# Softmax times V: the last head of each pass is normalised inside the loop's final branch, with stores of its own in the last pass

## The chip, the cores and the metric

The kernel runs on one core of one Trainium2 chip. The metric is device microseconds of one execution. A core has five engines that run their own instruction streams and wait for each other through semaphores: PE (TensorE, matmuls; PEld is its weight load), DVE (VectorE), ACT (ScalarE), POOL (GpSimd) and SP (SyncE, which here issues DMAs). Sixteen DMA engines move data between the chip's main memory and the on-chip memory.

## The reference

For 8 x 12 = 96 heads, each with a 1024 x 1024 matrix of scores and a 1024 x 64 matrix V, all in float32:

```python
scores_max = np.max(scores, axis=-1, keepdims=True)
attn = np.exp(scores - scores_max)
attn = attn / (np.sum(attn, axis=-1, keepdims=True) + 1e-8)
return np.matmul(attn, v).astype(np.float32)
```

## The kernel before

**Tiling.** A head's 1024 rows of scores are laid over 128 partitions, 8 rows in each, so that a head is one load of 4 MB with 32 KB in a row per partition. The text calls these 8 slices of 128 rows "rows" r = 0 to 7. The loop (L434) takes AHEAD = 4 heads a pass, in 24 passes; the four heads of a pass stand in slots k = 0 to 3, and each slot has its own buffer of scores, s_nat0 to s_nat3.

**One row.** ScalarE takes the exponential (L386, two rows in one instruction, in slot 3 from row 2 on one row) without subtracting the maximum. PE transposes the row in eight matmuls of 128x128 (L399), DVE copies the result out of PSUM (L406), and PE multiplies it with V in eight matmuls (L165). V carries a column of ones, so the row's sum comes out beside the product. The products lag three rows behind the transposes (LAG). Four rows share one PSUM bank, so that a head has two banks, b = 0 and 1.

**Normalising.** When the fourth row of a bank is done, DVE takes the reciprocal of the sums (L144) and multiplies (L150, two instructions of 64 partitions) into out_sb. One out_sb holds two heads, and one store of 512 KB writes it out.

**The check.** Because no maximum is subtracted, the kernel watches that the sums and V stay within bounds: a maximum over V for each slot, at row 4 (L257), and a few operations on 128x1 tiles; the result is a count that is read after the loop. If it is not full, general() (from L300) computes everything again in the careful way; with these inputs it is branched over.

**The order of the DMAs.** All DMAs are issued by SP, in an order written out by hand (queue() chains them). In a pass: load 0 and load 1 for the next pass (L352, each after ScalarE has read the slot; switched off in the last pass), the store of heads 0 and 1, and then last() (L355), which has three branches. In passes 0 to 21: load 2, the V for the pass after the next, load 3, the store of heads 2 and 3. In pass 22, the next to last: load 2 in two halves, three rows of load 3, the store, and the rest of load 3 as (2, 1, 1, 1) rows. In pass 23: the store of heads 2 and 3 in three parts, the last bank apart. Every DMA tells of its completion on one of eight semaphores that are handed around in turn; where the branches differ, the one that has fewer DMAs adds to the semaphore itself, so that the counts are the same at the end of each branch.

Of the kernel before, what the change touches and what calls it, by code (L numbers as in the profile page):

```python
# [22 lines left out]
EPS = 1e-8  # L23
# [3 lines left out]
def kernel(  # L27
# [65 lines left out]
    p_bufs = buffers(sb_pool, 8, [P, EB, SK], FP16, "p_nat")  # L93
    pt_bufs = buffers(sb_pool, 4, [P, SK], FP16, "pt")
    out_bufs = buffers(sb_pool, 2, [P, T, R, D], FP32, "out_sb")
    seen = const_pool.tile([P, 1 + AHEAD * R + 1], FP32, name="seen")
    nc.vector.memset(seen, 1.0)
    v_seen = const_pool.tile([P, 1 + AHEAD + 1], FP32, name="v_seen")
    nc.vector.memset(v_seen, 1.0)
    psT_bufs = buffers(ps_pool, 4, [P, SK], FP16, "psT")  # L100

# [34 lines left out]
    def one(bh, n):  # L136
        return bh[bass.ds(n, 1)].rearrange("o p r d -> (o p) r d")

    def normalise(k, st, b, behind=None):

        psO = st["psO"][b][:, 0 : G * M].rearrange("p (g m) -> p g m", m=M)
        at = 1 + k * R + b * G
        recip = seen[:, at : at + G].rearrange("p (g o) -> p g o", o=1)
        inverse = nc.vector.reciprocal(out=recip, in_=psO[:, :, D : D + 1])  # L144
        if behind is not None:
            after(inverse, behind)
        h = k % T
        for t in range(T):
            part = slice(t * W, (t + 1) * W)
            nc.vector.tensor_tensor(  # L150
                out=st["out_sb"][h * W : (h + 1) * W, t, b * G : (b + 1) * G, :],
                in0=psO[part, :, 0:D],
                in1=recip[part].to_broadcast([W, G, D]),
                op=mybir.AluOpType.mult,
            )

    def finish(u):

        n0, k, r, pt, st = u
        b, g = r // G, r % G  # L160
        if r == 0:
            st["out_sb"] = out_bufs[k // T]
        bank = st["psO"][b]
        for c in range(C):
            product = nc.tensor.matmul(  # L165
                out=bank[:, g * M : (g + 1) * M],
                lhsT=pt[:, c * P : (c + 1) * P],
                rhs=st["vones"][:, c, 0:M],
                start=(c == 0),
                stop=(c == C - 1),  # L170
            )
            in_line(product)
        if g == G - 1 and (b > 0 or k < AHEAD - 1):
            normalise(k, st, b)
        if r == R - 1:
            spread_v(k)
            if k == T - 1:
                store(n0, 0)

    def store(n0, k, whole=True):  # L180

        to = out_bh.rearrange("(m x) y -> m x y", x=P)[bass.ds((n0 + k) // T, 1)]
        to = to.rearrange("o x (t b y) -> (o x) t b y", t=T, b=R // G)
        of = out_bufs[k // T][:].rearrange("x t (b g) d -> x t b (g d)", g=G)
        parts = [(slice(0, T), slice(0, R // G))]
        if not whole:
            parts = [(slice(0, T), slice(0, R // G - 1))]
            parts += [(slice(t, t + 1), slice(R // G - 1, R // G)) for t in range(T)]
        for t, b in parts:
            dma = nc.sync.dma_start(out=to[:, t, b, :], in_=of[:, t, b, :])  # L190
            for other in stores:
                apart(dma, other)
                apart(other, dma)
            apart(dma, dma)
            stores.append(dma)
            queue(dma)

    stores = []
    writers = {}
# [36 lines left out]
    def spread_v(k):  # L236

        for s in range(S):
            spread = nc.gpsimd.tensor_copy(  # L239
                out=vones_bufs[k][s * Q : (s + 1) * Q, :, 0:D].rearrange(  # L240
                    "i (h l) d -> i h l d", l=L
                ),
                in_=v_sb[k * Q : (k + 1) * Q, :, s],
            )
            for watch in watches:
                apart(spread, watch, "products in between")
                apart(watch, spread, "products in between")

    def spread_of(tile, n):

# [30 lines left out]

    def small(name, dtype=FP32):
        turn[name] = turn.get(name, 0) + 1
        return const_pool.tile([P, 1], dtype, name=f"{name}{turn[name]}")

    count = const_pool.tile([1, 1], I32, name="count")
    fits, right = small("fits"), small("right", FP16)

    def judge(bank):
# [9 lines left out]

    def general():  # L300

        s, x = s_bufs[0], s_bufs[1]
        out_n = out.rearrange("b h (p r) d -> (b h) p r d", p=P)
        v_n = v.rearrange("b h (c p) d -> (b h) p c d", p=P)
        lift, den = small("lift"), small("den")
        p_row, pt = x[:, 0, :], x[:, 1, :]
        v1 = x[:, 2, 0 : C * M].rearrange("p (c m) -> p c m", m=M)
        nc.vector.memset(x[:, 2, 0 : C * M], 1.0)
        half = SK // 2
        with tc.For_i(0, BH, 1) as n:  # L310
            nc.sync.dma_start(out=s[:], in_=one(sc_bh, n))
            for c in range(C):
                nc.sync.dma_start(
                    out=v1[:, c, 0:D],
                    in_=v_n[bass.ds(n, 1)].rearrange("o p c d -> (o p) c d")[:, c, :],
                )
            with tc.For_i(0, R, 1) as r:
                row = s[:, bass.ds(r, 1), :].rearrange("p o j -> p (o j)")
                nc.vector.tensor_reduce(out=lift, in_=row, axis=X, op=ALU.max, negate=True)
                nc.scalar.activation(out=p_row, in_=row, func=EXP, bias=lift[:])  # L320
                for c in range(C):
                    at = c * P % half
                    nc.tensor.transpose(
                        out=psO_bufs[c * P // half][:, at : at + P],
                        in_=p_row[:, c * P : (c + 1) * P],
                        identity=ident32[:],
                    )
                for h in range(2):
                    nc.vector.tensor_copy(out=pt[:, h * half : (h + 1) * half], in_=psO_bufs[h][:, 0:half])
                for c in range(C):  # L330
                    nc.tensor.matmul(
                        out=psO_bufs[2][:, 0:M],
                        lhsT=pt[:, c * P : (c + 1) * P],
                        rhs=v1[:, c, :],
                        start=(c == 0),
                        stop=(c == C - 1),
                    )
                nc.vector.tensor_scalar(
                    out=den, in0=psO_bufs[2][:, D : D + 1], scalar1=EPS, scalar2=None, op0=ALU.add
                )  # L340
                nc.vector.reciprocal(out=den, in_=den)
                nc.vector.tensor_scalar(
                    out=out_bufs[0][:, 0, bass.ds(r, 1), :].rearrange("p o d -> p (o d)"),
                    in0=psO_bufs[2][:, 0:D], scalar1=den[:], scalar2=None, op0=ALU.mult,
                )
            nc.sync.dma_start(
                out=out_n[bass.ds(n, 1)].rearrange("o p r d -> (o p) r d"), in_=out_bufs[0][:, 0]
            )

    def load_next(k, n0):  # L350
# [1 line left out]
        if k < AHEAD - 2:  # L352
            load(k, (n0 + (AHEAD + k)) % BH, cond=n0 < BH - AHEAD)

    def last(n0):  # L355


        before = queued[-1:]

        with tc.If(n0 < BH - 2 * AHEAD) as cmp:  # L360
            queued[:] = before
            load(AHEAD - 2, (n0 + (2 * AHEAD - 2)) % BH)
            load_v((n0 + 2 * AHEAD) % BH)
            load(AHEAD - 1, (n0 + (2 * AHEAD - 1)) % BH)
            store(n0, AHEAD - T)
        with cmp.Else():
            with tc.If(n0 < BH - AHEAD) as cmp2:
                queued[:] = before
                load(AHEAD - 2, BH - 2, (4, 4))
                load(AHEAD - 1, BH - 1, (3,))  # L370
                store(n0, AHEAD - T)
                load(AHEAD - 1, BH - 1, (2, 1, 1, 1), 3)
            with cmp2.Else():
                queued[:] = before
                store(n0, AHEAD - T, whole=False)

    def heads(n0):

        for k in range(AHEAD):
            st = dict(vones=vones_bufs[k], psO=[take(psO_bufs) for b in range(R // G)])  # L380
            for r in range(R):
# [23 lines left out]
                pt = take(pt_bufs)  # L405
                copy = nc.vector.tensor_copy(out=pt[:], in_=psT[:])  # L406
                rewrite(pt, copy)
                if k == AHEAD - 1 and r == R - 1:

                    normalise(k, st, 0, copy)  # L410
                if r == G:
                    watch_v(k, copy)
                    if k == AHEAD - 1:
                        spread_of(v_seen, AHEAD)
                        within(fits, v_seen, AHEAD, V_MIN, V_MAX)
                if r == R - 1:
                    load_next(k, n0)
                pending.append((n0, k, r, pt, st))
# [1 line left out]
                    finish(pending.pop(0))  # L420
        while pending:
            finish(pending.pop(0))
        spread_of(seen, AHEAD * R)
        judge(st["psO"][-1])
        last(n0)

    assert BH % AHEAD == 0 and BH >= 2 * AHEAD and SK == Q * S * C
    load_v(0)
# [2 lines left out]
    for k in range(AHEAD):  # L431
        spread_v(k)
    load_v(AHEAD)
    with tc.For_i(0, BH, AHEAD, iteration_sync="reg_based") as n0:  # L434
        queued.clear()
        line.clear()
        heads(n0)
# [34 lines left out]
```

## Time and profile before

| | |
|---|---|
| median of 3 runs | 1073.61 us (1073.51 to 1074.58) |
| the profiled execution's own time | 1074.27 us |
| its span, first to last instruction | 1072.4 us |
| PE, PEld busy | 728.2 us (68%), 694.7 us (65%) |
| DVE busy | 776.4 us (72%) |
| ACT busy | 740.4 us (69%) |
| POOL busy | 244.9 us (23%) |
| moved by DMA | 453.09 MB, mean 423 GB/s |
| granted TensorE clock, mean | 0.815 |

Times in the profile are microseconds from the span's start. A busy share is an average over the span; what bounds a stage is seen from what its engines wait for. In a row of the order of time, the numbers are the start and the length, then the engine, the line of the kernel, the operation, out<-in, the shapes, the count of instructions merged, and in brackets the idle time before it with what seems to have ended it. A small q behind an engine's name means its sequencer (waits, branches, issues), not the engine itself.

### The profile page before, as it was taken

The page shows a single profiled execution, that of the slowest core. Times are in us where ns is not written, and L with a number is a line of the kernel's source. Part 1 is how long each engine was busy: PE and PEld are TensorE (multiplying, and loading weights), DVE is VectorE, ACT ScalarE, POOL GpSimd, SP SyncE. Part 2 cuts the span into 40 slices and gives each one's busy share as a digit, 9 for nine tenths or more (in the row PEclk, how much of TensorE's full clock was granted, in tenths as well). Part 3 has the DMA queues.
Part 4 walks back from the last instruction along what each step waited for, and adds up shares of the span by engine and source line. Part 5 has one row for each costly group of instructions (what it writes and reads, how often), then busy time and mean ns, then how long its engine had stood idle before and what let it go on. Part 6 is the DMA issues. An engine that isn't in the chain of part 4 may idle for free.

```text
span 1072.4 us, 33178 instructions
## 1 busy us (share of the span) xinstructions
PE 728.2 (68%) x12312; PEld 694.7 (65%) x12312; DVE 776.4 (72%) x1663; ACT 740.4 (69%) x480; POOL 244.9 (23%) x406
## 2 busy tenths in 40 slices
PE   2766766766766668676666766667767667667685
PEld 2665766666766667676666766666766667666574
DVE  1876776877767777777686776767767778677686
ACT  3766776766858667676666676766857667686684
POOL 3113112131121211221113112131121211222113
PEclk9887878878888788878887878878787788877888
DMA  9999999999999999999999999999999999999993
GB/s 395 433 417 431 428 439 431 430 425 438 433 433 431 429 433 423 438 430 430 430 429 432 430 433 431 430 431 432 426 441 431 433 430 429 432 423 438 430 423 139
DMA packets 25336, 453.09 MB, mean 423 GB/s; under 512 B 2800, under 2 KB 3312, under 8 KB 9712
## 3 DMA queue, kind: packets, MB, share of 16 engines
q1 hardware_dynamic: 25328, 453.00, 98.6%
q8 instruction: 4, 0.07, 0.0%
q14 instruction: 4, 0.03, 0.0%
HBM read 436.21 MB, written 25.17 MB: 430 GB/s over the span
## 4 chain that ended last, share of the span: by engine, by line
DMA 60%; PE 10%; PEld 6%; issue 6%; ACT 6%; DVE 5%; POOL 3%; SPq 1%; POOLq 1%; DVEq 0%; ACTq 0%; PEldq 0%
DMA s_nat<-in_scores_dram 60%; PE psT L399 6%; ACT p_nat L386 6%; PE psO L165 4%; PEld L399 4%; POOL vones L239 3%; PEld L165 2%; DVE pt L406 2%; DVE v_seen L257 1%; SPq L230 1%; SPq L218 0%; POOLq L239 0%; DVE v_seen L251 0%; DVE part L270 0%; POOLq L360 0%
## 5 line engine op out<-in xcount | busy, mean ns | idle before, releaser
L386 ACT ACTIVATE p_nat<-s_nat 128x2048 f16<-128x2048 f32 (+1 forms) x456 | 709.7, 1631 | 223.2 <-DMA s_nat<-in_scores_dram 176.6
L399 PE MATMUL psT<-order,p_nat 128*128 128x128 f16 x6144 | 571.0, 251 | 240.9 <-ACT p_nat L386 228.5
L406 DVE COPY pt<-psT 128x1024 f16<-128x1024 f16 x768 | 520.7, 687 | 221.8 <-PE psO L165 87.2
L399 PEld LDWEIGHTS <-p_nat 128*128 128x128 f16 x6144 | 462.1, 125 | 259.3 <-ACT p_nat L386 246.2
L239 POOL CAST vones<-v_sb 32x512 f16<-32x512 f32 x400 | 244.2, 610 | 819.3 <-PE L399 506.7
L165 PE MATMUL psO<-vones,pt 128*128 128x65 f16 x6144 | 360.0, 205 | 32.8 <-DVE v_seen L251 15.4
L165 PEld LDWEIGHTS <-pt 128*128 128x128 f16 x6144 | 301.9, 106 | 44.7 <-DVE pt L406 30.2
L150 DVE TENSOR_TENSOR out_sb<-psO,seen 64x256 f32<-64x256 f32 x384 | 161.9, 422 | 53.7 <-DMA out_dram<-out_sb 43.1
L386 ACT ACT_TABLE_LOAD x24 | 30.8, 1283 | 94.7 <-PE psO L165 49.9
L257 DVE TENSOR_REDUCE v_seen<-vones 128x1 f32<-128x512 f16 x96 | 65.6, 684 | 2.2
L294 PE MATMUL psO<-vones,right 128*1 128x1 f16 x24 | 3.9, 164 | 62.7 <-DVE right L278 62.7
L294 PEld LDWEIGHTS <-right 128*1 128x1 f16 x24 | 1.9, 79 | 65.7 <-DVE right L278 65.7
L144 DVE RECIPROCAL seen<-psO 128x4 f32<-128x4 f32 x192 | 33.8, 176 | 0.9 <-PE psO L165 0.2
L298 DVE CAST count<-psO 1x1 int32<-1x1 f32 x24 | 3.5, 146 | 6.1 <-PE psO L294 6.1
L274 DVE SCALAR_TENSOR_TENSOR part<-seen,fits 128x1 f32<-128x1 f32 x24 | 7.0, 291 | 0.8
L251 DVE TENSOR_REDUCE seen<-seen 128x1 f32<-128x33 f32 x24 | 4.5, 188 | 0.8
L278 DVE SCALAR_TENSOR_TENSOR right<-seen,part 128x1 f16<-128x1 f32 x24 | 4.2, 175 | 0.8
L252 DVE TENSOR_REDUCE seen<-seen 128x1 f32<-128x33 f32 x24 | 4.2, 176 | 0.0
L278 DVE SCALAR_TENSOR_TENSOR fits<-v_seen,part 128x1 f32<-128x1 f32 x24 | 3.6, 150 | 0.0
L252 DVE TENSOR_REDUCE v_seen<-v_seen 128x1 f32<-128x5 f32 x24 | 3.6, 148 | 0.0
L251 DVE TENSOR_REDUCE v_seen<-v_seen 128x1 f32<-128x5 f32 x24 | 3.5, 148 | 0.0
L270 DVE TENSOR_SCALAR part<-v_seen 128x1 f32<-128x1 f32 x24 | 3.5, 144 | 0.0
(10 smaller groups left out, 1.4 us busy)
## 6 DMA issues: line engine op xcount, KB each, us to landing
s_nat<-in_scores_dram SPq DMA_DIRECT2D x96, 4096.0 KB, 31.5
v_sb<-in_v_dram SPq DMA_DIRECT2D x24, 1024.0 KB, 18.8
out_dram<-out_sb SPq DMA_DIRECT2D x47, 512.0 KB, 26.3
s_nat<-in_scores_dram SPq DMA_DIRECT2D x2, 2048.0 KB, 32.3
s_nat<-in_scores_dram SPq DMA_DIRECT2D x1, 1536.0 KB, 32.6
s_nat<-in_scores_dram SPq DMA_DIRECT2D x3, 512.0 KB, 21.1
s_nat<-in_scores_dram SPq DMA_DIRECT2D x1, 1024.0 KB, 24.9
out_dram<-out_sb SPq DMA_DIRECT2D x1, 256.0 KB, 2.6
```

Of the source, the lines that this page charges most:

```text
L144: inverse = nc.vector.reciprocal(out=recip, in_=psO[:, :, D : D + 1])
L150: nc.vector.tensor_tensor(out=st["out_sb"][h * W : (h + 1) * W, t, b * G : (b + 1) * G, :], in0=psO[part, :, 0:D], in1=recip[part].to_broa ...
L165: product = nc.tensor.matmul(out=bank[:, g * M : (g + 1) * M], lhsT=pt[:, c * P : (c + 1) * P], rhs=st["vones"][:, c, 0:M], start=(c == 0) ...
L230: nc.sync.dma_start(out=v_sb[:].rearrange("x h s l d -> x (h s l d)"), in_=rows[bass.ds(n // AHEAD, 1)].rearrange("o x y -> (o x) y"),)
L239: spread = nc.gpsimd.tensor_copy(out=vones_bufs[k][s * Q : (s + 1) * Q, :, 0:D].rearrange("i (h l) d -> i h l d", l=L), in_=v_sb[k * Q : ( ...
L251: nc.vector.tensor_reduce(out=tile[:, 0:1], in_=tile[:, 0 : n + 1], axis=X, op=ALU.min)
L252: nc.vector.tensor_reduce(out=tile[:, n + 1 : n + 2], in_=tile[:, 1 : n + 2], axis=X, op=ALU.max)
L257: watch = nc.vector.tensor_reduce(out=v_seen[:, 1 + k : 2 + k], in_=vones_bufs[k][:, :, 0:D], axis=mybir.AxisListType.XY, op=ALU.max, appl ...
L278: nc.vector.scalar_tensor_tensor(out=out, in0=tile[:, 0:1], scalar=low, in1=part, op0=ALU.is_ge, op1=ALU.mult)
L386: exp = nc.scalar.activation(out=p_nat[:, g : g + rows, :].rearrange("p r (x v) -> p x r v", v=Q * L), in_=s_bufs[k][:, r + g : r + g + ro ...
L399: turned = nc.tensor.transpose(out=psT[:, c * P : (c + 1) * P], in_=p_row[:, c // L, c % L, :], identity=order16[:],)
L406: copy = nc.vector.tensor_copy(out=pt[:], in_=psT[:])
```

## The change

- In slot 3, normalise() is taken out of finish(). The reciprocal of bank 0 is put ahead of the last copy of the pass; the rest of the head's normalising is put into the branches of last(), which now stands before the check of the sums in place of behind it. In passes 0 to 22 it is the same work as before (rest()).
- In pass 23 a new function end() does it otherwise: ScalarE multiplies bank 0 in four instructions, DVE bank 1 in one instruction over all 128 partitions, and both write into s_nat0 (rows 0 and 1). Head 2's half of out_sb is stored by itself; bank 1 goes out by two stores on SP, bank 0 by two on ScalarE's own queue.
- The maximum over V of all four slots is taken in slots 0 and 1 (rows 3 and 6), and summed up in slot 2.
- In pass 22 the rest of load 3 goes as (1, 1, 1, 1, 1) rows in place of (2, 1, 1, 1).
- The loop's head is aligned for DVE and SP (head_align_engines).
- general() is written as one loop over rows in place of two nested ones, and uses s_nat0 alone. It does not run with these inputs.
- A few small tiles come from a pool of their own. A declaration that the maximum over V does not depend on the spreading of V is dropped, so that it now waits for it.

```diff
+    def end(st):
+        k, h = AHEAD - 1, (AHEAD - 1) % T
+        send(
+            nc.sync.dma_start(
+                out=out_bh[(BH - T) * W : (BH - T + h) * W],
+                in_=out_bufs[k // T][0 : h * W].rearrange("x t r d -> x (t r d)"),
+            )
+        )
+        to = out_bh[(BH - 1) * W : BH * W].rearrange("j (t b y) -> t j b y", t=T, b=R // G)
+        done = [s_bufs[0][:, b, 0 : G * D] for b in range(R // G)]
+        psO, recip = sums(k, st, 0)
+        for g in range(G):
+            nc.scalar.mul(done[0][:, g * D : (g + 1) * D], psO[:, g, 0:D], recip[:, g, :])
+        invert(k, st, 1)
+        psO, recip = sums(k, st, 1)
+        nc.vector.tensor_tensor(
+            out=done[1].rearrange("p (g d) -> p g d", d=D),
+            in0=psO[:, :, 0:D],
+            in1=recip.to_broadcast([P, G, D]),
+            op=ALU.mult,
+        )
+        for t in range(T):
+            part = slice(t * W, (t + 1) * W)
+            send(nc.sync.dma_start(out=to[t, :, 1, :], in_=done[1][part]))
+            send(nc.scalar.dma_start(out=to[t, :, 0, :], in_=done[0][part]), line=False)
...
-    def last(n0):
+    def last(n0, st):
         before = queued[-1:]
+        k = AHEAD - 1
+
+        def rest():
+            normalise(k, st, 0)
+            invert(k, st, 1)
+            normalise(k, st, 1)
 
         with tc.If(n0 < BH - 2 * AHEAD) as cmp:
             queued[:] = before
+            rest()
             load(AHEAD - 2, (n0 + (2 * AHEAD - 2)) % BH)
...
             with tc.If(n0 < BH - AHEAD) as cmp2:
                 queued[:] = before
+                rest()
                 load(AHEAD - 2, BH - 2, (4, 4))
                 load(AHEAD - 1, BH - 1, (3,))
                 store(n0, AHEAD - T)
-                load(AHEAD - 1, BH - 1, (2, 1, 1, 1), 3)
+                load(AHEAD - 1, BH - 1, (1, 1, 1, 1, 1), 3)
             with cmp2.Else():
                 queued[:] = before
-                store(n0, AHEAD - T, whole=False)
+                end(st)
...
+                if k < AHEAD // 2 and r in (G - 1, R - 2):
+                    watch_v(2 * k + (r > G), copy)
+                if k == AHEAD // 2 and r == 1:
+                    spread_of(v_seen, AHEAD)
+                    within(fits, v_seen, AHEAD, V_MIN, V_MAX)
                 if k == AHEAD - 1 and r == R - 1:
-
-                    normalise(k, st, 0, copy)
-                if r == G:
-                    watch_v(k, copy)
-                    if k == AHEAD - 1:
-                        spread_of(v_seen, AHEAD)
-                        within(fits, v_seen, AHEAD, V_MIN, V_MAX)
+                    after(copy, invert(k, st, 0))
...
+        last(n0, st)
         spread_of(seen, AHEAD * R)
         judge(st["psO"][-1])
-        last(n0)
...
-    with tc.For_i(0, BH, AHEAD, iteration_sync="reg_based") as n0:
+    aligned = [mybir.EngineType.DVE, mybir.EngineType.SP]
+    with tc.For_i(
+        0, BH, AHEAD, iteration_sync="reg_based", head_align_engines=aligned
+    ) as n0:
```

## The prediction

> **What bounds the kernel now.** I read the page's slices and queues first.
>
> ```profile
> DMA  9999999999999999999999999999999999999993
> q1 hardware_dynamic: 25328, 453.00, 98.6%
> ```
>
> The sixteen DMA engines are busy in every slice but the last. 453 MB at the slices' usual 430 GB/s is 1053 us of the span of 1072.4 us. No compute engine is above 72%. Only two things can therefore move the time: a hole in the DMA stream, or the end behind it. So the next view is the order of time of SP's queue, the only one that issues DMAs (start, length, what), over two passes of the loop.
>
> ```profile
> 949.53 5.03 SPq L218 DMA_DIRECT2D s_nat<-in_scores_dram  x2
> 966.47 0.36 SPq L190 DMA_DIRECT2D out_dram<-out_sb  x1
> 967.39 0.34 SPq L218 DMA_DIRECT2D s_nat<-in_scores_dram  x1
> 985.06 0.33 SPq L230 DMA_DIRECT2D v_sb<-in_v_dram  x1
> 985.77 0.33 SPq L218 DMA_DIRECT2D s_nat<-in_scores_dram  x1
> 986.41 0.35 SPq L190 DMA_DIRECT2D out_dram<-out_sb  x1
> 993.50 5.01 SPq L218 DMA_DIRECT2D s_nat<-in_scores_dram  x2
> ```
>
> One pass issues load 0 and load 1 (949.53), the store of heads 0 and 1, load 2, v, load 3, and the store of heads 2 and 3; then 993.50 is load 0 of the next pass. How long the DMAs of 985 to 987 took to land:
>
> ```profile
> s_nat<-in_scores_dram SPq DMA_DIRECT2D x1, 4096.0 KB, 28.2
> out_dram<-out_sb SPq DMA_DIRECT2D x1, 512.0 KB, 28.8
> ```
>
> Load 3, issued at 985.77, landed at 1014.0; the store of 986.41 landed at 1015.2. **Load 0 of the next pass was issued at 993.5, 21.7 us before the DMAs ahead of it had landed.** That lead keeps the stream without holes. Last, the end: ScalarE's order of time in the last two passes.
>
> ```profile
> 1001.89 7.32 ACT L386 ACTIVATE p_nat<-s_nat 128x2048 f16<-128x2048 f32 x4 [3.83 <-DMA s_nat<-in_scores_dram]
> 1014.09 7.60 ACT L386 ACTIVATE p_nat<-s_nat 128x2048 f16<-128x2048 f32 x7 [4.87 <-DMA s_nat<-in_scores_dram]
> 1034.77 10.92 ACT L386 ACTIVATE p_nat<-s_nat 128x2048 f16<-128x2048 f32 x6 [1.12 <-PE psT L399]
> 1045.95 6.60 ACT L386 ACTIVATE p_nat<-s_nat 128x2048 f16<-128x2048 f32 x4 [0.27 <-PE L399]
> 1053.55 4.85 ACT L386 ACTIVATE p_nat<-s_nat 128x1024 f16<-128x1024 f32 x5 [0.99 <-PE L399]
> ```
>
> A head that finds its data costs 7.3 us (slots 0 to 2) or 7.6 us (slot 3). In the last pass ScalarE works almost without a gap from 1034.8 to 1058.4, while the last loads still arrive. The very last row's load:
>
> ```profile
> L218 SPq DMA_DIRECT2D s_nat<-in_scores_dram x1: 328/328/328, 1036.2 to 1036.2; - x1
> DMA to landing us min/median/max: 21.1/21.1/21.1
> ```
>
> It landed at 1057.2, 1.2 us before the last exponential ended.
>
> **The change, part by part.**
>
> *1. A new wait in front of load 0.* end() writes its results into s_nat0 and stores them from there: two stores on SP, two on ScalarE's queue. Whoever refills s_nat0 must wait for them, and that is load 0 of the next pass. A DMA's completion is told by one of eight counters that the branches share, and a wait in the loop's head can't know which branch ran. From the built order of SP (L252 is the load; counters 0 to 7 are named DMAHW):
>
> ```
> before: DMACopy s_nat_79<-in_scores_dram [waits DMAHW0,Activation,...]
> after:  DMACopy s_nat_79<-in_scores_dram [waits DMAHW4,DMAHW5,DMAHW0,DMAHW6,DVE,DMAHW7,Activation,...]
> ```
>
> In end(), counters 4 to 7 belong to the four new stores; in the branch of the other passes, 4 is v, 5 is load 3 and 6 is the store of heads 2 and 3. The awaited counts are those of everything through the previous pass. So load 0 is issued only when load 3 and that store have *landed*: in the pass shown at 1015.2 instead of 993.5. They are the last things in the stream, and load 1, the next store, load 2, v and load 3 stand behind load 0 in SP's order. **The lead of 21.7 us becomes less than nothing: each pass the stream runs dry and starts again.** Loads issued in passes 1 to 22 pay it (pass 0 has nothing before it, in pass 23 the load is switched off): 22 times.
>
> The price of one hole: the rest of the landing, SP's wake-up, and the time from an issue to full rate. No row shows a load into an idle stream in mid-kernel. The nearest rows are a store into an idle stream, and the first load of all:
>
> ```profile
> out_dram<-out_sb SPq DMA_DIRECT2D x1, 512.0 KB, 2.7
> 1058.00:1058.20 0.20, 0.20 (x10) 0.20 (x8) 0.20 (x1) 0.20 (x1) 0.20 (x1) 1.00 0.00 0
> 1058.20:1059.70 1.50, 1.09 (x23) 0.84 (x19) 1.47 (x3) 0.20 (x1) 0.37 (x1) 1.00 0.86 350
> DMA to landing us min/median/max: 4.9/18.8/32.0
> ```
>
> The store (issued 1057.34, line two and three are stretches with the DMA share and GB/s last) moves nothing until 1058.2; 2.7 us less 1.2 us for 512 KB at 430 GB/s leaves 1.4 to 1.5 us. The first load of v took 4.9 us, less 2.4 us for 1 MB: 2.5 us, everything cold. SP's wake-up adds some 0.2 us (an estimate: three of its small steps of 0.06 us each stand between a landing and the issue). Bounds: 1.4 and 2.7 us. I take 1.9: a load from memory like the second row, but warm like the first. **22 x 1.9 = +41.8 us** (30.8 to 59.4).
>
> The Trainium skill (DMA: Bandwidth & Descriptors, Latency and other measured facts) gives about 0.6 us to the first byte on this path; the store's row shows 0.86, and with 0.6 the sum would be some 6 us less.
>
> At each hole all sixteen engines wait for the slowest. In the stretches after 1051 the DMA share falls from 0.38 through 0.18 to 0.06 at 1056: the engines finish over some 6 us. One that is slow throughout costs nothing new; where different ones are late in different passes, it adds. I take +2 us (0 to 4).
>
> *2. A fifth load for the last head.* (2,1,1,1) rows become five single ones. Alone this would let row 3 start 1.2 us earlier and hide. But with nine DMAs in that branch the counters wrap: in the built order row 7's load counts on DMAHW3, which load 2 of that branch already uses. ScalarE's first exponential of slot 2 waits for DMAHW3 through the whole previous pass, and its exponential of row 7 has no DMA wait any more. So **in the last pass ScalarE does not begin head 94 before the last row of head 95 has landed** (L). Behind it everything of heads 94 and 95 stands in line. Before: last exponential over at L + 1.2. After: L + 0.1 + 7.3 + 7.6 = L + 15.0.
>
> *3. The end itself.* Taken out of the last head: a maximum over v (0.69 us on DVE) and four small operations (some 0.6), now in slots 0 to 2, where DVE has gaps; two multiplies of 0.42 us and one reciprocal move to ScalarE (four multiplies, which no row shows; from the 1.04 us of a 128x1024 exponential under 1 us together) and lie beside DVE's last products; bank 1 takes one multiply in place of two (0.43 for 0.86). From the last exponential to the end of the loop it was 1058.4 to 1066.3, 7.9 us. Now: transposes 0.6, copy 0.7, products 0.7, reciprocal and multiply 0.65, two issues on SP 0.8, landing 1.9 (the last store's row), SP's last steps 0.3: 5.6, and up to 1 us because DVE (0.63 a copy, 1.05 a half head) is behind after two heads at ScalarE's rate: 6.4. So the loop ends at L + 21.4, where it ended at L + 9.1: **+12.3 us** (9 to 14).
>
> *4. The way out.* Behind the loop SP and DVE branch over general():
>
> ```profile
> L440 SPq COMPARE_BRANCH  x2: 46/48/49, 1067.4 to 1068.0; - x2
> L439 SPq FUSED_REGOPS  x1: 181/181/181, 1070.8 to 1070.8; - x1
> ```
>
> Nothing runs on SP from 1068.0 to 1070.8. general() becomes shorter (185 instructions on SP for 237) and the loop's head is aligned on both engines. I take the stall as gone, with five semaphore steps of 0.07: **-2.9 us** (0 to -3.1). The Trainium skill (Runtime: NRT & Kernel Launch, Instruction fetch mechanics) says that a taken branch to code outside the two pages held makes the engine fetch first; that fits the gap, and if the target still lies outside, this term is nothing.
>
> *5. At nothing:* the order in each pass of DVE's normalising (moved into the branch), and ScalarE's new wait for it at the loop's head. DVE's end would be about 12 us after the hole begins, load 0 lands 1.9 + 9.7 after it; the half microsecond is hidden by ScalarE's 3.8 and 4.9 us of waiting for loads. Without that cover it would cost up to 2 us a pass.
>
> **Sum.** 41.8 + 2 + 12.3 - 2.9 = +53.2 us on a span of 1072.4, and 1.9 us lie around the span of that execution (1074.27): 1127.5. The median of the runs shown is 0.7 below that execution: **1127 us**.
>
> **Rivals.**
> *The hole is there, the last pass is not held* (I misread the counter): the end is then shorter by 5 us or so in place of longer: 41.8 + 2 - 5 = +39, 1112 us. For it: the trace can't show the counter. Against: row 7's exponential has no other wait that makes it safe.
> *The last pass is held, the hole isn't*: for it, 98.6% says that queued work hides late issues; against it, the wait is for landing, and nothing is queued behind it. 12.3 - 2.9: 1083 us.
> *Neither: the change does what it looks like.* The end loses DVE's 1.3 us, half of the last multiplies, one store issue and the branch stall: some 5 us, **1068 us, faster**. It decides if load 0 is still issued more than 2 us before the store ahead of it lands.
> *The hole is deeper* (over 2.7 us each, SP's list of waits slow): from 3 us on, 1151 us and more.
>
> **How the numbers follow.** Forecast 0.82, hole alone 0.06, last pass alone 0.05, neither 0.03, deeper 0.04. The bounds of the terms give 1110 to 1151 for the forecast; its ends need all terms on one side, so I cut the top and let the bottom reach the hole alone: 1108 to 1146. A measurement of this kernel tells about 0.2% (2 us). Faster 0.03, same 0.01, slower 0.96.
>
> **What would show it.** Load 0 issued just after the landing of the store before it, and DMA stretches near 0 once a pass, some 46 us apart: right; load 0 still 20 us ahead: step 1 wrong. ScalarE idle for some 15 us before head 94: step 2; heads 94 and 95 begun before L: wrong. SP without the 2.8 us gap: step 4. If the holes are there and the time is still under 1100, their price is what I got wrong.

## The result and the profile after

The changed kernel takes 1159.57 us (median of 4 runs, 1158.64 to 1160.12). The kernel before, on the same chip, takes 1073.67 us. The ratio is 1.0796 (95% interval 1.0779 to 1.0813): **slower by 86 us**. The forecast of 1127 us had the direction right, but the time lies above its range. The profiled execution has a span of 1158.3 us; its own lines are below. (Of one kernel further down, cover4, the four executions fall into two groups 28 us apart.)

The page first: the share of time in which the main DMA queue is busy, over the 40 slices and in total.

```profile
DMA  9998999999999999999999999999999999999991
q1 hardware_dynamic: 25152, 452.87, 93.9%
```

The bytes are nearly the same as before, but the share fell from 98.6% to 93.9%. In slices of 29 us that hardly shows: a hole of 3 us in a slice still leaves a 9. One has to look at the order of time of SP's queue (start, length, what):

```profile
1005.49 0.33 SPq L252 DMA_DIRECT2D s_nat<-in_scores_dram  x1
1006.07 0.35 SPq L193 DMA_DIRECT2D out_dram<-out_sb  x1
1038.45 1.23 SPq L252 DMA_DIRECT2D s_nat<-in_scores_dram  x2
...
1052.24 0.33 SPq L264 DMA_DIRECT2D v_sb<-in_v_dram  x1
1052.87 0.33 SPq L252 DMA_DIRECT2D s_nat<-in_scores_dram  x1
1053.45 0.35 SPq L193 DMA_DIRECT2D out_dram<-out_sb  x1
1085.69 1.23 SPq L252 DMA_DIRECT2D s_nat<-in_scores_dram  x2
```

The view of line 193 in the stretch around 1006 tells when that store landed:

```profile
DMA to landing us min/median/max: 32.2/32.2/32.2
```

The store issued at 1006.07 landed at 1038.24, and 0.21 us later, at 1038.45, SP issues load 0 (the "x2" is load 0 and load 1). Before the change load 0 was issued 21.7 us *ahead* of that landing. From 1038.45 to 1085.69 a pass takes 47.24 us; the mean pass took 43.9 before.

What the DMA engines do around 1038.45, in stretches (length, five engines' busy time, clock, then DMA share and GB/s; a packet counts where it starts, so the stretch in which ten 32-KB packets start has a share over 1):

```profile
1036.00:1037.00 1.00, 0.00 (x0) 0.00 (x0) 0.46 (x1) 0.00 (x0) 0.00 (x0) 1.00 0.78 320
...
1037.50:1038.00 0.50, 0.00 (x0) 0.00 (x0) 0.00 (x0) 0.50 (x1) 0.00 (x0) 1.00 0.15 57
1038.00:1038.40 0.40, 0.00 (x0) 0.00 (x0) 0.04 (x1) 0.40 (x1) 0.00 (x0) 1.00 0.00 0
1038.40:1038.80 0.40, 0.00 (x0) 0.00 (x0) 0.38 (x1) 0.40 (x1) 0.00 (x0) 1.00 0.00 0
1038.80:1039.20 0.40, 0.13 (x2) 0.13 (x3) 0.39 (x1) 0.40 (x2) 0.00 (x0) 1.00 0.00 0
1039.20:1039.60 0.40, 0.40 (x7) 0.40 (x7) 0.04 (x1) 0.40 (x1) 0.00 (x0) 0.55 3.09 821
```

Nothing moves from 1037.91 to 1039.42. The records of the single packets show the same stretch without a packet, 1.50 to 1.53 us long, 22 times, once for each load 0 of passes 1 to 22.

Then the end. ScalarE's order of time:

```profile
1130.66 14.82 ACT L423 ACTIVATE p_nat<-s_nat 128x2048 f16<-128x2048 f32 x11 [14.86 <-DMA s_nat<-in_scores_dram]
1149.30 0.93 ACT L218 ACTIVATE s_nat<-psO,seen 128x64 f32<-128x64 f32 x4 [3.82 <-PE L172]
```

ScalarE stands idle for 14.86 us and then does heads 94 and 95 in one go. The last row landed at 1130.56 (call that moment L, as in the prediction). Behind the last exponential (over at 1145.48) VectorE is the one that is late:

```profile
1145.38 0.69 DVE L443 COPY pt<-psT 128x1024 f16<-128x1024 f16 x1 [0.18 <-PE L436]
1146.11 0.88 DVE L157 TENSOR_TENSOR out_sb<-psO,seen 64x256 f32<-64x256 f32 x2
1147.01 1.94 DVE L443 COPY pt<-psT 128x1024 f16<-128x1024 f16 x3
1149.22 0.69 DVE L443 COPY pt<-psT 128x1024 f16<-128x1024 f16 x1 [0.18 <-PE L172]
```

It still has head 94's second half and four copies to do, 4.4 us of work, where the kernel before had 2.9 us from its last exponential to the end of its last copy. Last, the way out (count, length in ns, first and last start):

```profile
L479 SPq COMPARE_BRANCH  x2: 46/48/49, 1155.9 to 1156.2; - x2
...
L478 SPq FUSED_REGOPS  x1: 178/178/178, 1156.7 to 1156.7; - x1
```

The gap of 2.75 us behind SP's branch is 0.55 us now.

Four moments of each profiled execution are enough to compare the kernels:

| kernel | L | last exponential over, from L | last store landed, from L | end of the span, from L | span |
|---|---|---|---|---|---|
| before | 1057.2 | 1.2 | 8.8 | 15.2 | 1072.4 |
| after | 1130.6 | 14.9 | 24.0 | 27.8 | 1158.3 |
| own_tiles | 1052.7 | 14.9 | 23.8 | 27.6 | 1080.3 |
| four_loads | 1132.8 | 1.3 | 8.1 | 11.9 | 1144.7 |
| both | 1053.7 | 1.3 | 9.3 | 13.1 | 1066.8 |
| before_five | 1057.1 | 14.9 | 24.4 | 30.7 | 1087.7 |
| before_addr | 1052.1 | 1.3 | 9.8 | 16.2 | 1068.2 |

L is 73.3 us later after the change, and the way from L to the end 12.6 us longer.

### The profile page after: what moved, and what is told of

The parts are those of the page before. It is cut to its first block, busy times and chain, and to the rows that moved or that the text cites. A ratio compares the mean times of both kernels' runs of the same rounds, so it can differ in the third digit from the quotient of the medians.

```text
span 1158.3 us, 33473 instructions
## 1 busy us (share of the span) xinstructions
PE 735.0 (63%) x12312; PEld 696.8 (60%) x12312; DVE 790.8 (68%) x1660; ACT 741.1 (64%) x484; POOL 244.1 (21%) x406
## 3 DMA queue, kind: packets, MB, share of 16 engines
q1 hardware_dynamic: 25152, 452.87, 93.9%
## 4 chain that ended last, share of the span: by engine, by line
DMA 66%; PE 10%; PEld 6%; ACT 4%; DVE 4%; issue 3%; POOL 3%; SPq 1%; POOLq 1%; ACTq 0%
DMA s_nat<-in_scores_dram 66%; PE psT L436 5%; PE psO L172 5%; ACT p_nat L423 4%; DVE pt L443 4%; PEld L436 4%; POOL vones L273 3%; PEld L172 3%; SPq L264 1%; SPq L252 0%; POOLq L273 0%; POOLq L395 0%; POOLq L471 0%; POOLq L506 0%; ACTq L423 0%
## 5 line engine op out<-in xcount | busy, mean ns | idle before, releaser
L436 PE MATMUL psT<-order,p_nat 128*128 128x128 f16 x6144 | 577.8, 252 | 325.9 <-ACT p_nat L423 324.6
L311 DVE SCALAR_TENSOR_TENSOR right<-seen,part 128x1 f16<-128x1 f32 x24 | 10.8, 449 | 0.8
L311 DVE SCALAR_TENSOR_TENSOR fits<-v_seen,part 128x1 f32<-128x1 f32 x24 | 10.2, 426 | 0.0
L307 DVE SCALAR_TENSOR_TENSOR part<-seen,fits 128x1 f32<-128x1 f32 x24 | 4.0, 168 | 0.8
```

Source lines behind the costliest of these rows:

```text
L311: nc.vector.scalar_tensor_tensor(out=out, in0=tile[:, 0:1], scalar=low, in1=part, op0=ALU.is_ge, op1=ALU.mult)
L436: turned = nc.tensor.transpose(out=psT[:, c * P : (c + 1) * P], in_=p_row[:, c // L, c % L, :], identity=order16[:],)
```

## The experiments

**Which parts of the change cost.** Four kernels take the two suspected costs away one by one, or put one of them into the kernel before.

*own_tiles*: results in tiles of their own.

```diff
-        done = [s_bufs[0][:, b, 0 : G * D] for b in range(R // G)]
+        done = [done_bufs[b][:] for b in range(R // G)]    # two new tiles of [P, G * D]
```

> The changed kernel with one difference: end() writes its results into two small tiles of their own and no longer into s_nat0. Load 0 then has no wait for load 3 and for the store before it, and its lead comes back. Theory (the holes cost 3.5 us each, 22 of them, as the 47.27 us between two loads 0 against 43.77 show; the held last pass costs the rest): no stretch without DMA in the loop, L back at about 1057, last exponential still at L + 14.9, end at L + 27.7: about 1086 us. Rival A (a hole costs 1.9 us as predicted, and some 35 us come from the new order of VectorE's work in each pass): 1118 us. Rival B (the passes became longer because of ScalarE's wait for VectorE at the loop's head, not because of load 0): little change, over 1140 us.

Measured: 1082.42 us (1081.99 to 1082.88), ratio to before 1.0079 (1.0062 to 1.0096). SP's order of time again has load 0 far ahead of the landing of the store in front of it (982.78 is that store, 989.67 load 0 and load 1):

```profile
982.14 0.33 SPq L253 DMA_DIRECT2D s_nat<-in_scores_dram  x1
982.78 0.35 SPq L194 DMA_DIRECT2D out_dram<-out_sb  x1
989.67 5.03 SPq L253 DMA_DIRECT2D s_nat<-in_scores_dram  x2
```

No stretch without packets is left in the loop. So the tile that end() writes into is worth **1159.57 - 1082.42 = 77.2 us, 3.5 us for each of 22 holes**. Rivals A (1118) and B (over 1140) are out. The time is some 4 us below the theory's 1086, since L came not at 1057 but at 1052.7; that is taken up below (before_addr).

*four_loads*: `load(AHEAD - 1, BH - 1, (2, 1, 1, 1), 3)` in place of `(1, 1, 1, 1, 1)`.

> The changed kernel with one difference: the last five rows come as (2,1,1,1) as before, eight DMAs in that branch and not nine, so that row 7's load has a counter for itself. Theory: the holes stay (47.3 us a pass); ScalarE begins head 94 before the last row has landed, and the end is some 16 us nearer to L (27.7 us less 13.7 of ScalarE and less 2 to 3 of VectorE's backlog): about 1143 us. Rival (the counter isn't what holds ScalarE): ScalarE still idle until L, 1159 us.

Measured: 1146.97 us (1146.4 to 1148.14), ratio 1.0682 (1.0664 to 1.07): 12.6 us less than the changed kernel. ScalarE doesn't wait for L (1132.8) any more:

```profile
1110.88 17.48 ACT L423 ACTIVATE p_nat<-s_nat 128x2048 f16<-128x2048 f32 x10 [1.90 <-PE L172]
1129.24 4.85 ACT L423 ACTIVATE p_nat<-s_nat 128x1024 f16<-128x1024 f32 x5 [0.88 <-PE L172]
```

It is over at L + 1.3, as before the change. The end came 15.9 us nearer to L, as expected; L itself was 2.3 us later in this execution.

*both*: the two edits together.

> Both of these differences at once: tiles of their own and (2,1,1,1). What is left of the change is the normalising in the branch, the whole-bank end with own stores, the checks of v in the first heads, the shorter general() and the aligned loop head. Theory: no holes, no held last pass; the stall on the way out (2.6 us) and about 1 us of VectorE's work are saved: 1069 to 1071 us. Rival (the order of VectorE's work or ScalarE's wait at the loop's head costs by itself): over 1074 us.

Measured: **1068.07 us (1067.64 to 1068.66), ratio to before 0.9943 (0.9926 to 0.996)**. What is left of the change is an improvement of 6 us against the kernel before. The rival, a price of VectorE's new order, is out. The four kernels make a square: the holes cost 77.2 us with the held last pass and 78.9 without (1146.97 - 1068.07); the held last pass costs 12.6 with the holes and 14.4 without (1082.42 - 1068.07). The two add up within 2 us.

*before_five*: the kernel before with five single rows.

> The kernel before with one difference: the last five rows as five loads of one row. Theory (nine DMAs wrap the eight counters, and ScalarE's first exponential of slot 2 waits for row 7): ScalarE idle until L, last exponential at L + 14.9, the end 14 to 17 us later: about 1088 us. Rival (the counter matters only with the other parts of the change): ScalarE begins head 94 as before, 1072 to 1074 us.

Measured: 1089.43 us (1089.07 to 1089.6), ratio 1.0142 (1.0125 to 1.0159), 15.3 us slower by this one line. ScalarE in its last pass:

```profile
1057.16 14.82 ACT L386 ACTIVATE p_nat<-s_nat 128x2048 f16<-128x2048 f32 x11 [15.06 <-DMA s_nat<-in_scores_dram]
```

The same wait as in the changed kernel, without anything else of the change. As expected.

*whole_load2*: tiles of its own, five single rows, but `load(AHEAD - 2, BH - 2, (8,))` for `(4, 4)`, so that the branch has eight DMAs and no counter is used twice.

> Tiles of its own, five single rows as in the changed kernel, but load 2 of that branch in one piece instead of two: eight DMAs in the branch, so that no counter is used twice. Theory (the held last pass comes from the ninth DMA, not from five single rows): ScalarE begins head 94 before the last row lands, as in the kernel 'both': 1067 to 1069 us. Rival (five single rows hold ScalarE by themselves): 1082 us.

Measured: 1071.45 us (1070.93 to 1071.6), ratio 0.9972 (0.9962 to 0.9983). So five single rows hold nothing by themselves: it is the ninth DMA. The theory's 1067 to 1069 was missed by 2.5 us: ScalarE now waits until 1042.16 for the whole of load 2, where with (4,4) it could start on half of it, and the last exponential is over at L + 3.8 instead of L + 1.3.

**Is it the wait, or the empty stream?**

*in_slot1*: as the changed kernel, but `s_bufs[1]` for `s_bufs[0]` in end(). The wait is in front of load 1 then, with load 0 queued ahead of it.

> The changed kernel with one difference: end() writes its results into s_nat1 and not s_nat0. The same wait for load 3 and for the store before it now stands in front of load 1, with load 0 (4 MB, 9.7 us of stream) issued ahead of it. Theory (what costs is that the stream runs dry; a wait with work queued behind it costs nothing): no stretch without DMA in the loop, as with tiles of its own: about 1082 us. Rival (the wait as such costs, on SP's queue or as delay of what stands behind load 1): holes or dents of some microseconds once a pass, over 1110 us.

Measured: 1082.55 us (1081.88 to 1082.73), ratio 1.0074 (1.006 to 1.0087). This is own_tiles within 0.2 us. SP does wait, 22 us between load 0 and load 1, and the queue's share on the page is that of own_tiles (97.8%):

```profile
990.11 22.15 SPq L252 DMA_DIRECT2D s_nat<-in_scores_dram  x2
```

```profile
q1 hardware_dynamic: 25152, 452.87, 97.7%
```

Here a wait of 22 us costs nothing, with 9.7 us of stream queued behind the transfer waited for. The price comes from the queue that runs empty, not from the wait.

**How much cover does a hole need?** In cover1, cover2 and cover4 end() writes into rows 6 and 7 of s_nat0, and load 0 goes out as (1, 7), (2, 6) or (4, 4) rows. The first piece doesn't wait and covers the start of the second. first_row has the split (1, 7) without the cover, the results staying in rows 0 and 1.

```diff
-            load(k, (n0 + (AHEAD + k)) % BH, cond=n0 < BH - AHEAD)
+            load(k, (n0 + (AHEAD + k)) % BH, (1, 7) if k == 0 else (8,), cond=n0 < BH - AHEAD)
```

> The changed kernel with two differences: end() writes its results into rows 6 and 7 of s_nat0, and load 0 is issued as one row (512 KB) and seven rows. The row has no wait for the DMAs ahead and stands in the stream behind them: a cover of 1.2 us (512 KB at 432 GB/s) for the latency of the seven rows. Theory (a hole costs 3.5 us a pass, of it some 2.9 at the hole itself): 1.2 us less in each of 22 passes, period about 46.1 us, 1133 us. Rival (the hole's price doesn't depend on queued work, as the stream stops once in any case): 1159 us.

> The changed kernel with one difference: load 0 is issued as one row and seven rows, the results of end() stay in rows 0 and 1 of s_nat0, so that the first row waits for the store ahead just as the whole load did. It is cover1 without its cover. Theory (cover1 gained by the queued row, not by the split): period 47.2 us as in the changed kernel, 1159 us. Rival (the split as such shortens the start): 1135 us as in cover1.

Measured: cover1 1135.03 us (1133.86 to 1136.06), ratio 1.0567 (1.0551 to 1.0583); first_row 1180.14 us (1179.76 to 1185.11), ratio 1.1003 (1.0978 to 1.1027). The mean pass (v's issues, over the loop) is 46.05 us in cover1, 47.18 in the changed kernel and 48.04 in first_row. One row of 1.2 us ahead gave 1.13 us a pass back against the changed kernel, as the theory has it, and 2.0 against the kernel with the same split. first_row itself is 20 us slower than expected, 0.9 us a pass: its rival fell, and its theory too. The trace has sixteen steps of the semaphore for each DMA, taken here as one from each engine. In first_row the last engine ends the store ahead of a hole 0.3 to 3.1 us behind the first, 1.4 on average and over 2 us in 7 of 22 holes; in the changed kernel it is 0.6 on average. As bytes missing ahead of the hole that is 1.1 us a pass for 0.45, so 0.7 of the 0.9 us. The split alone doesn't bring it about, since in cover1, with the same split, the average is 0.6 too. What makes an engine late in first_row isn't shown, so the 2.0 us are an upper bound for what the cover gives.

> The same with load 0 as two rows and six: a cover of 2.4 us. Theory: 2.4 us less a pass, period about 44.9, 1106 us. Rival (a hole costs 1.9 us as predicted, and the other 1.6 us a pass come from elsewhere in the pass): the cover takes all of 1.9, 1118 us.

> As cover1 and cover2, with load 0 as four rows and four: a cover of 4.9 us. Theory (a hole is over once the cover is longer than the 3.5 us, and cover2 is slow because its two-row piece comes out uneven among the DMA engines): 1082 to 1086 us. Rival (splitting the load ahead of the wait costs by itself beyond one row): over 1110 us.

cover2: 1167.0 us (1163.94 to 1169.53), ratio 1.0866 (1.0845 to 1.0888). It should have been near 1106 and came out slower than the changed kernel; **both expectations failed**. The stretches around the landing that SP waits for (762.31 in its trace):

```profile
760.00:761.00 1.00, 0.00 (x0) 0.00 (x0) 0.00 (x0) 0.00 (x0) 0.00 (x0) 0.95 0.97 410
761.00:762.00 1.00, 0.00 (x0) 0.00 (x0) 0.00 (x0) 0.86 (x1) 0.00 (x0) 0.50 0.24 98
762.00:763.00 1.00, 0.00 (x0) 0.00 (x0) 0.53 (x2) 1.00 (x2) 0.00 (x0) 0.50 0.06 25
```

A share of 0.06 is one engine of sixteen. It is still on its packets of the store and of the two rows when the others have long finished both; SP waits for it, and the cover is used up before load 0's second piece is issued. This is so in nearly every pass of cover2: the last engine is 2.6 to 3.8 us behind the first in 21 of 22 stores ahead of that wait, which is longer than the cover of 2.4 us. Small pieces aren't needed for such a lag. Streams that never stop have it too: 2.8 to 5.9 us in the kernel before, 2.6 to 3.2 in own_tiles, 2.3 to 3.7 in in_slot1. In the changed kernel the holes let the late engines catch up (2.5 us ahead of the first hole, 0.3 to 1.3 ahead of the others). So a cover has to last for the lag of the slowest engine as well as for the 1.5 us without packets; that cover2 stays too short for this reason is read from its trace and not tried by itself. cover4's executions took 1085.63, 1112.69, 1113.76 and 1114.22 us. The first is within the theory's 1082 to 1086, the others are over the rival's 1110. It stays undecided. What stands is in_slot1 (cover 9.7 us: nothing left of the holes) and cover1 (1.2 us: 1.1 to 2.0 us of each).

*no_store01*: the changed kernel without the store of heads 0 and 1 in each pass, run once.

> The changed kernel without the store of heads 0 and 1 in each pass (these heads are not written). It asks about the second dent of each pass: 19 us behind the hole, in the last 3 us of load 1 and right before this store, the 32-KB packets take 1.4 to 2.1 us instead of 1.21, about 0.6 us lost a pass. Theory A (it belongs to the store that follows): no slow packets there, the period shorter by 1.2 (the store's own share) and 0.6: 45.5 us, about 1118 us. Theory B (it belongs to the distance from the hole): slow packets still some 18 us behind the hole, period 46.05, about 1131 us.

Measured: 1127.64 us (one execution), between the two. The slow packets are still there, but 39 us behind the hole, right before the other store of the pass. In this execution they go with the first store after the hole, not with a distance from it; what they cost wasn't saved, only moved. What makes these packets slow is open.

**Where the 6 us of "both" come from.**

*before_addr*: the small tiles from a pool allocated last, in the kernel before.

```diff
-    seen = const_pool.tile([P, 1 + AHEAD * R + 1], FP32, name="seen")
+    small_pool = ctx.enter_context(tc.tile_pool(name="small", bufs=1))
+    seen = small_pool.tile([P, 1 + AHEAD * R + 1], FP32, name="seen")     # v_seen, count and the rest too
```

> The kernel before with one difference: the small tiles (seen, v_seen, count and so on) come from a pool of their own that is allocated last, as in the changed kernel. The four score buffers then start at byte 21504 of each partition (a multiple of 512) instead of 21920 (416 bytes beyond one). Theory (the 4 us by which the last row lands sooner in the kernel 'both', 1053.7 for 1057.2, come from where the DMAs write): the last row lands at about 1053.5, the sixteen engines end within 3 us and not 6, about 1070 us. Rival (they come from the order of VectorE's work or of SP's queue): no change, 1074 us.

Measured: 1069.95 us (1068.88 to 1070.16), ratio 0.9954 (0.994 to 0.9968). As expected, by addresses alone. The score buffers, V's buffer and out_sb all move by the same 416 bytes, and the small tiles go behind them; which of these counts wasn't separated. The last stretches of the stream, first of the kernel before, then of before_addr (the last two columns):

```profile
1050.00:1052.00 2.00, 1.81 (x37) 1.55 (x35) 1.94 (x4) 2.00 (x2) 1.22 (x2) 1.00 0.68 274
1052.00:1054.00 2.00, 1.94 (x45) 1.78 (x43) 1.97 (x6) 1.00 (x2) 0.00 (x0) 1.00 0.22 90
1054.00:1056.00 2.00, 1.53 (x30) 1.26 (x27) 1.97 (x4) 2.00 (x3) 0.04 (x1) 1.00 0.07 27
1056.00:1058.00 2.00, 1.88 (x38) 1.64 (x36) 1.91 (x6) 2.00 (x3) 1.82 (x4) 1.00 0.02 8
```

```profile
1048.00:1050.00 2.00, 1.79 (x43) 1.80 (x43) 1.97 (x6) 1.54 (x2) 0.00 (x0) 1.00 0.75 307
1050.00:1052.00 2.00, 1.43 (x34) 1.31 (x32) 1.97 (x4) 2.00 (x3) 0.19 (x1) 1.00 0.20 82
```

The stream fades some 2 us earlier, and its thin end, in which few engines still work, is shorter by about 3 us. The steps of the semaphores show where the thin end comes from. In the kernel before three engines end each DMA some 2.8 us behind the first, and a fourth falls behind by about 0.25 us a pass until it is the last, 5.9 us behind. In before_addr three are 2.4 to 2.8 us behind; the fourth loses only about 0.09 us a pass and never becomes the last. In the kernel "both" a slow engine loses 0.09 us a pass too, but starts among the late ones and ends 4.2 us behind.

*before_align* (`head_align_engines` alone) and *before_general* (the shorter general() alone):

> The kernel before with one difference: the loop's head is aligned on VectorE and SP. Theory A (the 2.6 us that the way out lost in the kernel 'both' come from the alignment): from the last landing to the end 3.8 us and not 6.4, about 1071.5 us. Theory B (they come from the shorter general() that the branch jumps over): no change, 1074 us.

> The kernel before with one difference: the shorter general(), which isn't executed with these data. Theory A (the alignment): no change, 1074 us. Theory B (the shorter general()): the gap of 2.8 us on SP between its branch and the assertion is gone, about 1071.5 us.

Measured: before_align 1073.62 us, ratio 0.9993 (0.9984 to 1.0002); before_general 1074.43 us, ratio 0.9999 (0.999 to 1.0008). Neither can be told from no change. The traces say more. In before_align SP's gap behind the branch is 0.55 us, and from the last landing to the end of the span it is 4.2 us for 6.4. But its last row landed at 1059.2, 2.0 us later than in the kernel before: its slow engine becomes the last eight passes earlier and ends 7.7 us behind the first. What is gained on the way out is lost there; whether the alignment has to do with that isn't shown. In before_general the gap is gone:

```profile
L436 SPq COMPARE_BRANCH  x2: 46/48/49, 1066.8 to 1067.1; - x2
```

```profile
L435 SPq FUSED_REGOPS  x1: 181/181/181, 1067.3 to 1067.3; - x1
```

Its median span is 1069.8 us, some 3 us less than that of the kernel before; but its time lies 4.7 us above its span, where 1.8 us is the rule for every other kernel here. Two packets of 8 KB of an instruction queue stand at 1070.4 and 1073.1 in its trace, behind the end of the span at 1068.9; in the kernel before such packets stand at 1068.7 and 1071.4, around its gap. So the stall wasn't removed, it seems to have fallen behind the end of the span. A shorter span was no shorter time. The two edits together weren't tried on the kernel before.

## Why the prediction fell short, point by point

**Step 1, the new wait of load 0: the mechanism was right, its price was not.** Load 0 is issued 0.2 us behind the landing of the store ahead of it, 22 times, with the DMA share at zero once a pass, just as the working said. The step that failed is "The price of one hole: ... I take 1.9", with the "+2 us (0 to 4)" for unequal engines beside it: together 43.8 us, measured 77.2 (own_tiles), which is over the upper bounds of both terms too (59.4 and 4). The rival that I gave 0.04, "from 3 us on, 1151 us and more", is what happened, though not for the reason named there: SP's list of waits took the 0.2 us that I had put down.

What I priced was the stretch without packets. It measures 1.51 us: 0.33 from the last packet to the landing, 0.21 to the issue, 0.97 from there to the first packet. That agrees with the store's row, which I had read as 1.4 to 1.5 us plus 0.2. What I left out lies on both sides of it. Averaged over the 22 holes and counted as bytes missing against 433 GB/s, a hole costs 2.9 us, not 1.5: some 0.45 us before it, as the engines don't end together; and the first 32-KB packet of most engines (13 of 16 in the hole shown) takes 1.8 to 2.3 us where later ones take 1.21. A further 0.8 us is lost 19 us behind each hole, where some 24 packets, just before the next store, take 1.4 to 2.1 us. 2.9 + 0.8 = 3.7 us against a stream at a steady 433 GB/s; own_tiles falls short of that by 0.1 us a pass itself, so this is about the 3.5 us measured. In the terms of the sum: from the last packet to the full rate it is 2.4 us and not 1.9; the unequal ends are 22 x 0.45 = 10 us and not 2; and the slow packets at the next store, 0.8 us a pass, weren't in the sum. The row of the first load of all (2.5 us) was the nearer one, since it contains a first packet of a load from memory; I took a value nearer to the store's row.

The Trainium skill (DMA: Bandwidth & Descriptors, Anatomy of one DMA), there for DMAs that GpSimd issues, puts a fixed cost of about 2.0 us on each and most of that into the confirmation of the last write. The trace agrees neither in size nor in split: the landing follows the store's last packet by 0.33 us, as far as its packet records tell, and the larger parts are the start and the slow first packets. With 2.0 us a hole the 22 holes would have come to 44 us, as wrong as mine.

**Step 2, the ninth DMA: right.** ScalarE was predicted to start at L and to end at L + 15.0; it ended at L + 14.9. before_five shows the wait in the kernel before by that line alone, whole_load2 shows it gone with eight DMAs.

**Step 3, the end: mis-sized by 2.8 us.** From the last exponential to the end of the loop I had 6.4 us with "up to 1 us because DVE is behind". VectorE was 4.4 us behind, and the last store landed 9.1 us after the last exponential. From L to the end of the loop it is +15.1 us (24.2 for 9.1) and not +12.3. Up to the end of its last copy the sum had 0.6 + 0.7 + 1 = 2.3 us, and it took 4.4; the steps behind that (6.4 - 2.3 = 4.1 in the sum) took 4.8. So the term goes wrong mainly by the backlog. With the hold the kernel before (before_five) needs 9.5 us from the last exponential to the last landing, the changed one 9.1.

**Step 4, the way out: right in this kernel.** The gap went from 2.75 to 0.55 us, and from the last landing to the end of the span it is 3.8 us instead of 6.4: -2.6 for the predicted -2.9. That either of its two causes brings time by itself wasn't shown.

**Step 5, "at nothing": right for what it named, and one edit was not in the list.** The normalising in the branch and ScalarE's wait at the loop's head cost nothing that own_tiles or both would show. But moving the small tiles into a pool of their own moved the four score buffers from byte 21920 to byte 21504 of each partition, V's buffer and out_sb along with them, and that is a gain: L 3.5 us earlier in both than in the kernel before, 4.6 us of time in before_addr. I had read that edit as a change of names.

In the profiled executions L is 77.9 us later in the changed kernel than in own_tiles (the holes) and 4.5 earlier in own_tiles than before (put down to the addresses, since before_addr alone has 5.1); with 15.1 of end and -2.6 of way out that makes the 85.9 us by which the span grew.

That both measures the 1068 us of the rival "neither" is luck. That rival had some 2 us of a shorter end beside the way out. In both, the 5.6 us of span are 3.5 of L and 2.6 of way out, less 0.5 of an end that isn't shorter: from the last exponential to the last landing it takes 8.0 us for 7.6.

## What to carry to other kernels

Before a temporary is put into a buffer that the loop refills, ask which load must then wait for it, in every pass, even if the write happens only in the last one. A kernel at the limit of its DMA stream pays for each time the queue runs dry, and more than the empty stretch shows: count the ends of the engines before it and the slow first packets after it; but a wait with enough work queued behind what it waits for can be free (22 us of waiting cost nothing in in_slot1). Enough means more than the lag of the slowest DMA engine, which was some 3 us here (cover2). And count the DMAs of a branch before splitting one more: the ninth shares a counter, and a wait on it can hold an engine for a transfer it doesn't need.

## What the runs showed of the hardware

- **Where the buffers of the DMAs lie matters.** With the score buffers at byte 21504 (a multiple of 512) instead of 21920, and the other big buffers moved alike, the kernel took 4.6 us less. In the loop the scores' packets of 32 KB took 1213 ns instead of 1215 on average, V's packets of 8 KB 309 instead of 313, and the slow engine lost about 0.09 us a pass instead of 0.25. The Trainium skill (DMA: Bandwidth & Descriptors, How a descriptor splits into AXI transactions) says that a piece that doesn't begin at a multiple of 256 bytes is fetched from the boundary below, with bytes that nobody uses; 21920 is 160 bytes beyond one, and so is out_sb, from which the stores read. The direction agrees with before_addr; for the loads, which write to these addresses, the section doesn't say it, and that this is the mechanism wasn't tried by other offsets.
- **In a stream that never stops the sixteen engines stay apart.** The last ended 2.8 to 5.9 us behind the first in the kernel before, 2.6 to 3.2 in own_tiles, but 0.3 to 1.3 at the holes of the changed kernel after the first. Where nothing waits for a landing at the head of the queue this is hidden; in front of such a wait it is paid each time (cover2, and some passes of first_row).
- **Slow packets came with the first store after a restart**, 1.4 to 2.1 us for 1.21, and moved to the other store when the first was left out (no_store01, one execution).
- **A stall can leave the span and stay in the time** (before_general: 4.7 us between span and time, 1.8 elsewhere).
